# Three of four weight folds ahead of the projections, the fourth from sums and differences of mirrored channels

## The chip, the core and the metric

One NeuronCore of a Trainium2 chip runs the program. It has TensorE (PE in the profile; its weight loads are PEld), VectorE (DVE), ScalarE (ACT), GpSimd (POOL) and SyncE (SP), which issues most DMAs, 16 DMA engines, and a PSUM of eight banks. The metric is the device time of one execution in microseconds; lower is better.

## What is computed

One step of a two-layer diffusion backbone in fp32: 1024 latent and 256 context tokens of 1024 channels. Layer 0 has two attention mixers (global, and windowed with sinks), layer 1 a Fourier mixer. Cut to what matters here:

```python
def fourier_mix(u):
    b, s, _ = u.shape
    ug = u.astype(jnp.float32).reshape(b, s, C_GROUPS, C_GROUP_DIM)   # 4 groups of 256 channels
    f = jnp.fft.fft2(ug, axes=(1, 3), norm="ortho")
    return jnp.real(f).reshape(b, s, C_WIDTH).astype(u.dtype)

def odd_mix(h, w_in, w_out):
    u, gate = jnp.split(h @ w_in, 2, axis=-1)
    return (fourier_mix(u) * jax.nn.silu(gate)) @ w_out

# per layer: m = silu(cond) @ ada_w + ada_b -> shift, scale, gate
#   x = x + gate * mixer(rms_norm(x, g) * (1 + scale) + shift); at the end a final rms_norm
```

The Fourier transform along a group's 256 channels is linear in `u = h @ w_u`. So the kernel applies it to the weight: for each of the four groups it multiplies the group's 256 columns of `w_u` by a 256 x 256 table (cosines of frequencies 0 to 128, sines of 1 to 127). This is a *fold*, and its result goes to DRAM (`wd`) until layer 1 reads it.

## The kernel before, in words

All products are fp32, most of them as three products of a high and a low part (`mm3`, `F32R`). Tokens come in ten tiles of 128 rows, channels in eight blocks of 128.

**Opening.** The string `PH0` is an order written out by hand: one letter and a number for each step, carried out by `first_step`. Inside it the DMAs that SP issues keep the order of the code; the order on the other engines is that of the tile framework's scheduler, fixed when the program is built, and each engine takes its instructions in that order. `f0` and `f1` load a fold's two weight tiles (`wuT`, 2 x 512 KB, in halves) and the table `fch`; `F00` to `F13` are the pieces of folds 0 and 1; `L0` to `L3` load modulation weights, `A` multiplies them (`ada`), `M` transposes a result (`modt`) and writes `moda` and `modb`; `x` loads token groups, `N` normalises them, `T` transposes one channel block (`xt`), `X` and `Y` modulate it; `w0` loads the key/value weights, `s0` splits them, `K` and `R` are the products with them (`kv0s` to `kv6s`); `G00` to `G11` store the results of folds 0 and 1. The `t` banks of PSUM, three of them, are shared by `xt`, `modt` and the early fold pieces.

**A fold piece** (`fold_piece(g, kb2, ...)`) makes two blocks of 128 input channels. Each block is two products added up in PSUM (one for each half `j` of the 256 group channels): 128 x 128 weights from `wu[j]` (tile names `w`), and 128 x 256 of the table (tile name `h`). The four products fill one bank (`wa`), which ScalarE empties; four pieces make a fold. A product in plain fp32 is two records in the trace, one for each pass. Early pieces (`first=True`) keep their result in `u` buffers; late ones store it at once.

**Attention.** Blocks of two heads go through scores (`sL`, `sB`, `sC`), softmax, transposes (`pt`), value products (`av`) and a store to DRAM (`od`). Between blocks a `Filler` with a credit per block puts in other work: projections, gates (`ga`), at last folds 2 and 3 (named in `FLATE`, cost `FC` a piece) and the first output projections (`oz`, a token tile at a time, two halves). An output projection needs its attention output (`od`), gates (`gd`) and softmax totals (`scd`) back from DRAM, in `proj_in`, where GpSimd multiplies the three; `load_to` starts it a step ahead. After the attention (`late[0]`) the rest of the projections is drained.

**Layer 1** then runs gates (`g1E`, `g1O`), Fourier products (`u`, `pc`, `ps`) and the last projections (`of`), the last one in three pieces of columns with its norm.

Of the kernel before, what the change touches and what calls it, by code (L numbers as in the profile page):

```python
# [17 lines left out]
P = 128  # L18
# [13 lines left out]
PH0 = """f0 S0 x0 N0 f1 L0 F00 F01 F02 F03 w0 L1 F10 F11 F12 F13 x1 A0 T0 T1 s0 M0 X0 X1 T2 L2 N1 K0 K1  # L32
 A1 T3 M1 G00 G01 G10 G11 L3 X2 X3 K2 K3 Y0 R0 Y1 R1 w1 S1 T4 A2 x2 N2 Y2 T5 M2 R2 X4 Y3 X5 R3
# [7 lines left out]
EF = 2  # L41
QPRE, HOLD, AHEAD = 0, 0, 1
# [15 lines left out]
FC, XF = 1.3, False  # L58
QE_Z = ("pt", "q", "w", "u", "p")
# [5 lines left out]
FLATE = "f2 f3"  # L65
# [74 lines left out]
def hybrid_step(ctx: ExitStack, tc: tile.TileContext, I, O):  # L140
# [85 lines left out]
    craw = sm.tile([P, 8, 2], F32, name="craw", bufs=1)  # L226
    sp.dma_start(craw, I["cT"])
    act.activation(cs, craw, AF.Tanh, scale=0.5)
    dve.scalar_tensor_tensor(out=cs, in0=cs, scalar=1.0, in1=craw, op0=ALU.add, op1=ALU.mult)
    dve.tensor_scalar(cs, cs, 0.5, None, op0=ALU.mult)  # L230
    csw = take("e", (P, 8, 32))
    pool.memset(csw.a, 0.0)
    dve.tensor_copy(csw[:, :, 0:2], cs)
# [297 lines left out]

    fold = {}

    def fold_load(g, parts=1):
        if "f" not in fold:
            fold["f"] = take("h", (P, 2, 256))
            sp.dma_start(fold["f"].a, I["fch"])
        wu = [take("w", (P, 1024)) for j in range(2)]
        for h in range(parts):
            cols = slice(h * (1024 // parts), (h + 1) * (1024 // parts))  # L540
            for j in range(2):
                sp.dma_start(wu[j][:, cols], I["wuT"][(2 * g + j) * P : (2 * g + j + 1) * P, cols])
        return wu
# [7 lines left out]
    def fold_piece(g, kb2, wu, first=False):  # L551
        f = fold["f"]
        acc = bank("t" if first else "g", f"wa{g}{kb2}")
        for i in range(2):
            c0 = (2 * kb2 + i) * P
            for j in range(2):
                pe.matmul(
                    acc[:, i * 256 : i * 256 + 256], wu[j][:, c0 : c0 + P], f[:, j, :], start=j == 0, stop=j == 1
                )
# [22 lines left out]
    def small_loads(i):  # L582
# [1271 lines left out]
    sp.dma_start(O["y"][7 * P : 8 * P, 0:512], yt[:, 0:512])  # L1854
# [109 lines left out]
```

## Time and profile before

| | |
|---|---|
| median of 3 runs | 1200.98 us (1199.07 to 1201.01) |
| the profiled execution | 1199.7 us, its span 1197.9 us |
| TensorE busy | 1161.1 us |
| VectorE, ScalarE, GpSimd busy | 842.1, 578.5, 329.2 us |
| granted TensorE clock, mean | 0.992 |
| moved by DMA | 168.81 MB, 141 GB/s |

How to read the rows: an engine, the line of the kernel, the operation, and output <- input by tile names. `x` counts instructions. In an order of time the first two numbers are the start and the length in us, and `[idle <-who]` says how long the engine had been idle and what ended that. Matmul records overlap, so that their spacing and not their length is what TensorE spends. In a table of stretches each engine's busy time stands with its count, then the granted clock, the DMA share and GB/s.

### The profile page before, as it was taken

The numbers are of one execution on the slowest core, as the hardware profiler recorded it, in microseconds if no ns is written. First come the engines' busy times: TensorE is split into PE (matmuls) and PEld (weight loads), VectorE is DVE, ScalarE is ACT, GpSimd is POOL, SyncE is SP. The second block draws the span as 40 slices with busy tenths as digits, with TensorE's granted clock in tenths as the row PEclk, the third lists the DMA queues.
The fourth block names the chain that finished last, engine by engine and source line by source line (L and its number), as shares of the span: only waits on it lengthen the run. The fifth ranks groups of instructions, "written<-read, shape, count | busy, mean of one in ns | idle before, by whom it ended". The sixth has DMA issues, their size and how long they took to land. (4 is left out here: it accounts for less than half of the span.)

```text
span 1197.9 us, 22049 instructions
## 1 busy us (share of the span) xinstructions
PE 1161.1 (97%) x8103; PEld 1038.0 (87%) x8103; DVE 842.1 (70%) x2000; ACT 578.5 (48%) x1159; POOL 329.2 (27%) x298
## 2 busy tenths in 40 slices
PE   7999999999999999999999989989999999999997
PEld 5787899999999998899989979878878888997886
DVE  3479787877677776678888978688756953467543
ACT  3343465666556555556666765533463224342211
POOL 2255644411323230010110135313112217345001
PEclk9899999999999999999999999999999999999999
DMA  9957512323623232354353588576214436264321
GB/s 321 365 190 258 176 44 77 94 80 102 158 69 97 76 95 84 92 128 113 86 144 90 151 255 240 188 234 206 86 33 155 142 106 186 81 210 147 120 105 54
DMA packets 129840, 168.81 MB, mean 141 GB/s; under 512 B 26298, under 2 KB 86454, under 8 KB 129732
## 3 DMA queue, kind: packets, MB, share of 16 engines
q1 hardware_dynamic: 127364, 159.01, 43.6%
q0 software_dynamic: 2368, 8.39, 2.1%
q8 instruction: 64, 1.05, 0.4%
q14 instruction: 44, 0.36, 0.1%
HBM read 123.19 MB, written 44.16 MB: 140 GB/s over the span
## 5 line engine op out<-in xcount | busy, mean ns | idle before, releaser
L1044 DVE TENSOR_TENSOR pt<-pt,pt 128x512 fp32r<-128x512 f32 (+1 forms) x264 | 171.1, 657 | 40.6 <-ACT pt L275 39.9
L275 ACT ACTIVATE pt<-pt 128x512 fp32r<-128x512 f32 (+1 forms) x264 | 146.7, 576 | 91.2 <-PE pt L1041 53.9
L1047 PE MATMUL av<-pt,u 128*128 128x256 f32 x1008 | 165.1, 287 | 0.0
L1041 PE MATMUL pt<-identr,p 128*128 128x128 f32 x1008 | 154.9, 272 | 0.7 <-ACT e L1026 0.4
L263 PE MATMUL q<-w,u 128*128 128x256 f32 x960 | 143.7, 287 | 0.2 <-ACT h L725 0.2
L1047 PEld LDWEIGHTS av<-pt,u 128*128 128x128 f32 x1008 | 137.8, 189 | 3.1 <-DVE pt L1044 0.3
L263 PEld LDWEIGHTS q<-w,u 128*128 128x128 f32 x960 | 126.7, 189 | 5.8 <-issue 0.8
L263 PE MATMUL ga<-u,w 128*128 128x512 f32 (+1 forms) x576 | 124.5, 361 | 0.4 <-DVE h L817 0.3
L1041 PEld LDWEIGHTS pt<-identr,p 128*128 128x128 f32 x1008 | 118.9, 140 | 6.9 <-ACT e L1026 0.6
L965 ACT ACTIVATE p<-p,nm 128x1280 f32<-128x1280 f32 (+1 forms) x80 | 95.4, 1193 | 58.1 <-DVE p L958 57.8
L263 PEld LDWEIGHTS ga<-u,w 128*128 128x128 f32 x576 | 93.9, 188 | 14.6 <-ACT e L1056 0.5
L281 POOL TENSOR_TENSOR w<-h,w 128x512 fp32r<-128x512 f32 x39 | 52.3, 1357 | 129.6 <-DVE w L277 98.2
L924 PE MATMUL sL<-u,q 128*128 128x512 f32 x256 | 82.4, 409 | 0.8 <-DMA q<-qd 0.8
L281 POOL TENSOR_TENSOR u<-h,u 128x512 fp32r<-128x512 f32 x24 | 33.7, 1411 | 159.2 <-ACT u L275 148.1
L965 ACT ACTIVATE p<-p,NM 128x640 f32<-128x640 f32 (+2 forms) x80 | 59.2, 740 | 33.5 <-DVE p L958 33.2
L924 PE MATMUL sC<-u,q 128*128 128x256 f32 x320 | 62.8, 296 | 2.4 <-DMA q<-qd 1.9
L958 DVE TENSOR_SCALAR_CACHE_REDUCE p<-sL 128x512 f32<-128x512 f32 x64 | 43.8, 684 | 25.8 <-PE sL L924 16.3
L263 PE MATMUL oz<-u,u 128*128 128x512 f32 x208 | 59.5, 396 | 1.7 <-DVE h L1239 1.7
L263 PE MATMUL oz<-u,w 128*128 128x512 f32 x192 | 58.2, 396 | 0.4 <-ACT w L275 0.4
L698 POOL TENSOR_TENSOR h<-h,rope 128x512 f32<-128x512 f32 (+1 forms) x18 | 21.6, 1199 | 126.3 <-ACT h L781 77.7
L958 DVE TENSOR_SCALAR_CACHE_REDUCE p<-sL,nm 128x512 f32<-128x512 f32 x64 | 47.7, 745 | 12.0 <-PE sL L924 11.1
L924 PEld LDWEIGHTS sC<-u,q 128*128 128x128 f32 x320 | 48.3, 189 | 5.6 <-DVE e L1058 1.8
(745 smaller groups left out, 2589.2 us busy)
## 6 DMA issues: line engine op xcount, KB each, us to landing
q<-qd SPq DMA_DIRECT2D x80, 256.0 KB
p<-i_ada_w SPq DMA_DIRECT2D x20, 512.0 KB
h<-i_w_in SPq DMA_DIRECT2D x40, 256.0 KB
h<-i_w_out SPq DMA_DIRECT2D x32, 256.0 KB
pt<-i_ada_w SPq DMA_DIRECT2D x15, 512.0 KB
qd<-pt SPq DMA_DIRECT2D x20, 256.0 KB
q<-i_ada_w SPq DMA_DIRECT2D x9, 512.0 KB
qd<-q SPq DMA_DIRECT2D x18, 256.0 KB
```

The lines of the kernel that those rows point to most:

```text
L263: pe.matmul(out, a, b, start=i == 0, stop=i == n - 1)
L275: act.activation(out, in_, AF.Copy)
L281: pick("lo" + lc, lc).tensor_sub(dst_l, src, dst_h)
L698: pick("rope", XE["rope"]).tensor_mul(t1.rearrange("p t h (b c) -> p t (h b) c", b=2), y.rearrange("p t h (b c) -> p t (h b) c", b=2), cb)
L924: pe.matmul(ps, q_at(q, s, hc), keys, start=s == 0, stop=s == 1)
L958: dve.tensor_scalar(p[i][:, end[i] : end[i] + n], ps, sign, last[i], op0=ALU.mult, op1=ALU.min, accum_out=c)
L965: act.activation(p[i][:, 0 : end[i]], p[i][:, 0 : end[i]], AF.Exp, bias=last[i], scale=-1.0, accum_out=SU[:, t, hd + i, 0:1],)
L1041: pe.transpose(tp[:, jj * 256 + i * P : jj * 256 + i * P + P], p[i][:, off : off + P], ident)
L1044: dve.tensor_sub(pt[:, 1, 0:n], tp[:, 0:n], pt[:, 0, 0:n])
L1047: pe.matmul(acc, vv, pt[:, s, jj * 256 : jj * 256 + 256], start=c + jj + s == 0, stop=c + jj == nt - 1 and s == 1,)
```

## The change

Five edits go together.

1. Fold 2 moves into `PH0`: its load behind the modulation weights `L0`, its pieces `F20` to `F23` among the first transposes, its two stores (`G20`, `G21`) behind the second group's steps. `EF` is 3, so that the whole table `fch` is given up after three folds.
2. Fold 3 stays late and is made otherwise. The host orders a group's channels as 0 to 128 and then 255 down to 129, in `wuT` and in the table's rows alike, so that row p of the second tile is the mirror of row p of the first. Cosines are even and sines odd under the mirror: so the 129 cosine columns need the sum of the two tiles alone, and the 127 sine columns their difference. GpSimd makes the sum and VectorE the difference, 512 columns at a time; a block is then one product of 129 columns and one of 127. Row 0 pairs channel 0 with channel 128, whose cosines alternate in sign, so VectorE adds -2 times channel 128 (the new small input `w128`) to the odd cosine columns of each block.
3. The load and the SiLU of the conditioning vector (`craw`) come behind fold 0's load.
4. `AHEAD` goes from 1 to 2: after the attention a projection's operands are fetched two steps ahead.
5. The last of the final two stores is issued by ScalarE's queue.

```diff
-PH0 = """f0 S0 x0 N0 f1 L0 F00 F01 F02 F03 w0 L1 F10 F11 F12 F13 x1 A0 T0 T1 s0 M0 X0 X1 T2 L2 N1 K0 K1
- A1 T3 M1 G00 G01 G10 G11 L3 X2 X3 K2 K3 Y0 R0 Y1 R1 w1 S1 T4 A2 x2 N2 Y2 T5 M2 R2 X4 Y3 X5 R3
+PH0 = """f0 S0 x0 N0 f1 L0 F00 F01 F02 F03 f2 w0 L1 F10 F11 F12 F13 x1 A0 T0 T1 s0 F20 M0 F21 X0 X1 T2 F22 F23 L2 N1 K0 K1
+ A1 T3 M1 G00 G01 G10 G11 L3 X2 X3 K2 K3 Y0 R0 Y1 R1 w1 S1 T4 A2 x2 N2 Y2 T5 M2 R2 G20 G21 X4 Y3 X5 R3
   K4 Y4 K5 A3 T6 Y5 M3 R4 X6 T7 R5 X7 Y6 K6 Y7 K7 R6 R7"""
...
-EF = 2
-QPRE, HOLD, AHEAD = 0, 0, 1
+EF = 3
+QPRE, HOLD, AHEAD = 0, 0, 2
...
+E_FO, E_FW = "d", "d"
...
-FLATE = "f2 f3"
+FLATE = "f3"
...
     def fold_piece(g, kb2, wu, first=False):
         f = fold["f"]
+        if not first and kb2 % 2 == 0:
+            cols = slice(kb2 * 256, kb2 * 256 + 512)
+            fold["e"] = take("h", (P, 512))
+            pool.tensor_add(fold["e"].a, wu[0][:, cols], wu[1][:, cols])
+            pick("fo", E_FO).tensor_sub(wu[1][:, cols], wu[0][:, cols], wu[1][:, cols])
         acc = bank("t" if first else "g", f"wa{g}{kb2}")
         for i in range(2):
-            c0 = (2 * kb2 + i) * P
+            c0, b0 = (2 * kb2 + i) * P, i * 256
+            if not first:
+                ec = (kb2 % 2 * 2 + i) * P
+                pe.matmul(acc[:, b0 : b0 + 129], fold["e"][:, ec : ec + P], f[:, 0, 0:129], start=True, stop=True)
+                pe.matmul(acc[:, b0 + 129 : b0 + 256], wu[1][:, c0 : c0 + P], f[:, 0, 129:256], start=True, stop=True)
+                continue
             for j in range(2):
                 pe.matmul(
                     acc[:, i * 256 : i * 256 + 256], wu[j][:, c0 : c0 + P], f[:, j, :], start=j == 0, stop=j == 1
...
         copy("wo", "a", wo, acc.rearrange("p (i f) -> p i f", i=2))
+
+        for i in range(0 if first else 2):
+            odd = wo[:, i, 1:129:2]
+            n = 8 * g + 2 * kb2 + i
+            pick("fw", E_FW).tensor_scalar(odd, odd, w128[:, n : n + 1], None, op0=ALU.add)
...
+            sp.dma_start(w128, I["w128"])
+            dve.tensor_scalar(w128, w128, -2.0, None, op0=ALU.mult)
...
     for op in PH0.split():
         first_step(op)
+        if op == "f0":
+            cond_vectors()
...
-    sp.dma_start(O["y"][7 * P : 8 * P, 0:512], yt[:, 0:512])
+    act.dma_start(O["y"][7 * P : 8 * P, 0:512], yt[:, 0:512])
...
+    fch = fch[np.concatenate([np.arange(129), 256 - np.arange(1, 128)])].reshape(2, 128, 256).transpose(1, 0, 2)
...
-        "wuT": w1[:, :1024].T,
+        "wuT": w1[:, mirror].T,
```

Three places show how the instructions move. On TensorE in the opening, from the last transpose of the second channel block on, before (`modt0` is the first modulation transpose, `xt02` and `xt03` channel blocks 2 and 3):

```order
L424 MATMUL xt01_316<-identr_85,u9_137 128x128
L516 MATMUL modt0_329<-identr_85,e40_309 128x128
L424 MATMUL xt02_344<-identr_85,u6_134 128x128
...
L467 MATMUL ada1_407<-pt30_234,e2_114 32x128 x2
L526 MATMUL kv0s_117<-w22_222,u41_334 128x256
```

and now:

```order
L427 MATMUL xt01_323<-identr_85,u9_138 128x128
L573 MATMUL wa20_336<-h3_118,w22_223 128x256
L573 MATMUL wa20_336<-h3_118,w23_224 128x256
...
L519 MATMUL modt0_343<-identr_85,e42_316 128x128
L573 MATMUL wa21_348<-h3_118,w22_223 128x256
L573 MATMUL wa21_348<-h3_118,w23_224 128x256
...
L529 MATMUL kv0s_112<-w24_229,u44_354 128x256
```

Piece `wa20` stands ahead of `modt0` and `wa21` between it and the first key/value product; `xt02`, and behind it `wa22` and `wa23`, follow that product now.

In SP's queue at the same place, before (`p19` is the last tile of `L0`, the `h` tiles are the key/value weights, `pt30` is the first of `L1`):

```order
L496 DMA p19_194<-i_ada_w 128x4x256
L296 DMA h24_224<-i_w_in0 128x2x256
L296 DMA h25_226<-i_w_in0 128x2x256
L296 DMA h28_230<-i_w_in0 128x2x256
L296 DMA h29_232<-i_w_in0 128x2x256
L496 DMA pt30_234<-i_ada_w 128x4x256
```

and now:

```order
L499 DMA p19_195<-i_ada_w 128x4x256
L548 DMA w22_223<-i_wuT 128x512
L548 DMA w23_224<-i_wuT 128x512
...
L299 DMA h26_231<-i_w_in0 128x2x256
L299 DMA h27_233<-i_w_in0 128x2x256
```

Fold 2's four half tiles stand ahead of the key/value weights and so of everything behind them.

On TensorE late in the attention, before (`wa20` is fold 2's first piece, `pt7_31`, `av7_30` and `sB6_30` are attention blocks):

```order
L1041 MATMUL pt7_310_9298<-identr_85,p895_9063 128x128 x4
L924 MATMUL sC6_30_9371<-u683_7045,q908_9176 128x256 x2
L996 MATMUL sB6_300_9378<-u681_7043,q908_9176 128x384 x2
L557 MATMUL wa20_9277<-h919_9252,w920_9254 128x256
L557 MATMUL wa20_9277<-h919_9252,w921_9255 128x256
...
L1041 MATMUL pt7_312_9310<-identr_85,p895_9063 128x128 x4
```

and now, there and 41 rows further on:

```order
L1068 MATMUL pt7_310_9340<-identr_85,p899_9100 128x128 x4
L569 MATMUL wa30_9317<-h923_9289,h933_9314 128x129
L570 MATMUL wa30_9317<-h923_9289,w925_9292 128x127
...
L1023 MATMUL sB6_301_9430<-u685_7080,q912_9213 128x384 x2
L1068 MATMUL pt7_312_9352<-identr_85,p899_9100 128x128 x4
...
L951 MATMUL sC5_30_9709<-u687_7082,q955_9511 128x256 x2
L951 MATMUL sC5_31_9753<-u687_7082,q955_9511 128x256 x2
L266 MATMUL oz00_9569<-u826_8507,w930_9308 128x512
```

Fold 3's first piece stands where fold 2's stood, its products are 129 and 127 columns wide, and the first projection `oz00`, which stood behind the first halves of block 5's transposes and all eight late pieces, now follows the scores `sC5_31`, with four pieces ahead of it.

More of the change, by code (lines that the diff above doesn't have):

```diff
@@ L224, in hybrid_step, with cond_vectors @@
     rope = cp.tile([P, 8, 96], F32, name="rope")
[L226 to L230, printed above, removed]
     csw = take("e", (P, 8, 32))
     pool.memset(csw.a, 0.0)
-    dve.tensor_copy(csw[:, :, 0:2], cs)
+    def cond_vectors():
+        craw = sm.tile([P, 8, 2], F32, name="craw", bufs=1)
+        sp.dma_start(craw, I["cT"])
+        act.activation(cs, craw, AF.Tanh, scale=0.5)
+        dve.scalar_tensor_tensor(out=cs, in0=cs, scalar=1.0, in1=craw, op0=ALU.add, op1=ALU.mult)
+        dve.tensor_scalar(cs, cs, 0.5, None, op0=ALU.mult)
+        dve.tensor_copy(csw[:, :, 0:2], cs)
     def rsqrt(name, v, n, mul, post=None, pw=False):
@@ L532, in hybrid_step @@
     fold = {}
+    w128 = cp.tile([P, 32], F32, name="w128")
     def fold_load(g, parts=1):
         if "f" not in fold:
-            fold["f"] = take("h", (P, 2, 256))
-            sp.dma_start(fold["f"].a, I["fch"])
+            whole = parts > 1
+            fold["f"] = take("h", (P, 2 if whole else 1, 256))
+            sp.dma_start(fold["f"].a, I["fch"] if whole else I["fch"][:, 0:1, :])
         wu = [take("w", (P, 1024)) for j in range(2)]
@@ L570, in fold_piece @@
             drop(wb)
+        if not first and kb2 % 2 == 1:
+            drop(fold["e"])
         if kb2 == 3:
@@ L1880 @@
     w1 = A["odd_w_in"][0]
+    mirror = np.concatenate([256 * g + np.concatenate([np.arange(129), 256 - np.arange(1, 128)]) for g in range(4)])
     n = np.arange(256)
     ang = 2 * np.pi * ((n[:, None] * np.arange(129)[None, :]) % 256) / 256
-    fch = np.concatenate([np.cos(ang), np.sin(ang[:, 1:128])], axis=1).reshape(2, 128, 256).transpose(1, 0, 2)
+    fch = np.concatenate([np.cos(ang), np.sin(ang[:, 1:128])], axis=1)
+    fch = fch[np.concatenate([np.arange(129), 256 - np.arange(1, 128)])].reshape(2, 128, 256).transpose(1, 0, 2)
     def tab(fn, pos, p, length, scale):
@@ L1936 @@
         "cv": np.stack([A["cache_v_a"][0, 0], A["cache_v_b"][0, 0]]).reshape(2, 256, 128),
-        "wuT": w1[:, :1024].T,
+        "wuT": w1[:, mirror].T,
+        "w128": w1[:, 128:1024:256].reshape(8, 128, 4).transpose(1, 2, 0).reshape(128, 32),
         "w_g1": w1[:, 1024:][:, chan],
```

## The prediction

> **What bounds the kernel now.** I read the page first, then the stretches of the span, then the orders of time in the three places that the change touches.
>
> ```profile
> span 1197.9 us, 22049 instructions
> PE 1161.1 (97%) x8103; PEld 1038.0 (87%) x8103; DVE 842.1 (70%) x2000; ACT 578.5 (48%) x1159; POOL 329.2 (27%) x298
> PE   7999999999999999999999989989999999999997
> ```
>
> TensorE is busy for 97% of the span: work taken from it is worth its own time, unless the engine then waits. Its slices below 9 lie at the start, about the 25th and at the end. So I split the span there.
>
> ```profile
> 20.00:30.00 10.00, 7.50 (x91) 4.90 (x89) 5.44 (x9) 2.35 (x5) 3.91 (x3) 0.89 1.10 348
> 30.00:40.00 10.00, 8.67 (x89) 6.92 (x89) 2.24 (x7) 3.33 (x7) 1.65 (x1) 0.77 1.06 382
> 40.00:50.00 10.00, 8.64 (x50) 7.06 (x50) 5.80 (x10) 3.11 (x6) 3.07 (x3) 0.66 1.09 379
> 50.00:60.00 10.00, 10.00 (x140) 8.94 (x140) 4.41 (x10) 4.11 (x7) 2.95 (x2) 1.00 1.05 334
> ...
> 70.00:80.00 10.00, 9.85 (x79) 9.15 (x78) 9.15 (x18) 4.62 (x8) 5.75 (x5) 1.00 0.25 74
> ...
> 100.00:120.00 20.00, 17.80 (x241) 14.54 (x242) 19.11 (x42) 4.22 (x10) 10.53 (x11) 1.00 0.85 276
> ...
> 690.00:740.00 50.00, 46.24 (x300) 41.98 (x300) 40.48 (x105) 32.52 (x76) 21.88 (x22) 1.00 0.89 265
> 740.00:800.00 60.00, 55.95 (x291) 46.69 (x290) 45.66 (x98) 25.12 (x59) 20.01 (x13) 1.00 0.63 201
> 800.00:900.00 100.00, 97.75 (x462) 79.32 (x461) 71.85 (x117) 44.93 (x83) 20.47 (x16) 0.99 0.38 120
> ```
>
> After the length stand busy TensorE, its weight loads, VectorE, ScalarE and GpSimd, then granted clock, DMA share and GB/s. From 20 to 50 us TensorE idles 5.2 us, runs at a clock of 0.89, 0.77 and 0.66, and the DMA share is above 1. From 100 to 120 us VectorE, busy 19.1 of 20, is the bound. From 690 to 800 us, where folds 2 and 3 and the first output projections lie between attention blocks, TensorE idles 7.8 us. From 800 us on it is the bound nearly alone.
>
> **The folds.** What does one cost?
>
> ```profile
> 10.76:21.70 10.94, 10.94 (x51) 9.31 (x50) 1.00 1.07 372
> ...
> 724.42 0.60 PE L1041 MATMUL pt<-identr,p 128*128 128x128 f32 x4
> 724.85 1.89 PE L557 MATMUL wa<-h,w 128*128 128x256 f32 x8
> ...
> L557 PE MATMUL wa<-h,w 128*128 128x256 f32 x64 | 15.3, 382 | 1.7 <-ACT pt L275 1.3 <-ACT h L275 0.4
> ```
>
> The first row counts line 557 alone between 10.76 and 21.70 us, where it runs back to back at full clock: 51 records in 10.94 us, 0.2145 us each. The 382 ns in the last row are the length of a record, which overlaps the next. The last row also says that folds 2 and 3 are 64 records: 32 for a fold, that is 32 x 0.2145 = **6.9 us** of TensorE each.
>
> *Fold 2 leaves the late stage:* -6.9 us.
>
> *Fold 3 streams 129 or 127 columns instead of 256.* No row has an fp32 product of that size with 128 weights. The nearest one is the transpose, 128 fp32 weights and 128 columns: four in 724.85 - 724.42 = 0.43 us, 0.108 us each. I take that: 32 x (0.2145 - 0.108) = **-3.4 us**. The bounds are 0, if the weights, whose load lasts 9.31/50 = 0.186 us in the first row, set the pace, and -3.4 us, half the stream. I choose the transpose's end since it loads as many fp32 weights.
>
> Fold 3 pays elsewhere: two GpSimd sums and two VectorE differences of 128x512, and eight small additions on VectorE.
>
> ```profile
> 23.84 1.27 POOL L281 TENSOR_TENSOR w<-h,w 128x512 fp32r<-128x512 f32 x1 [7.33 <-DVE w L277]
> ...
> 25.76 1.63 DVE L281 TENSOR_TENSOR w<-h,w 128x512 fp32r<-128x512 f32 x1
> ...
> 27.65 0.15 DVE L479 TENSOR_TENSOR modb<-modt,bT 128x4 f32<-128x4 f32 x1
> ...
> 30.99 0.69 DVE L439 TENSOR_TENSOR u<-h,u 128x512 fp32r<-128x512 f32 x1
> ```
>
> That is 2 x 1.27 us on GpSimd and 2 x 0.69 + 8 x (0.15 to 0.43) = 2.6 to 4.8 us (a 128x4 row here, a 128x512 cast at 23.33 below) on VectorE, which is busy 40.5 of 50 us there; beside it TensorE has the attention. I cost it at 0 as long as VectorE has its 9.5 idle us; without them it is 2.6 to 4.8. Row 25.76 shows a price more: a VectorE subtraction beside a GpSimd one takes 1.63 us instead of 0.69, so each sum may hold VectorE up by 0.9 us, 1.9 us in all, which its idle time covers as well.
>
> The Trainium skill ("SBUF — State Buffer", on the shared port pair) says that the two engines' shared port pair is an exclusive lock for an instruction; that rule speaks against sums on GpSimd, and by it up to 2 x 1.27 us of VectorE would be lost. The rows agree in kind, with 0.94 us a time.
>
> **Fold 2 in the opening.** Its 6.9 us come in between the first modulation sums and the first K/V products.
>
> ```profile
> 25.47 0.33 PE L516 MATMUL modt<-identr,e 128*128 128x128 f32 x1
> 28.01 1.09 PE L424 MATMUL xt<-identr,u 128*128 128x128 f32 x4 [2.21 <-DVE moda L484]
> ...
> 29.95 0.80 PE L526 MATMUL kv0s<-w,u 128*128 128x256 f32 x2 [0.28 <-ACT u L437]
> ...
> 38.72 0.33 PE L516 MATMUL modt<-identr,e 128*128 128x128 f32 x1 [0.38 <-ACT e L511]
> 40.42 0.51 PE L526 MATMUL kv0s<-w,u 128*128 128x256 f32 x2 [1.38 <-ACT u L437]
> ...
> 42.10 1.94 PE L424 MATMUL xt<-identr,u 128*128 128x128 f32 x8 [0.93 <-DVE u L418]
> ```
>
> The gaps up to 42.1 us are 2.21 + 0.28 + 0.38 + 1.38 + 0.93 = 5.2 us. They would hide most of 6.9 us, but not for free. Piece wa20 stands ahead of modt0: 8 x 0.2145 = 1.7 us and an eviction of 0.60 us (21.82 below), so modt0 comes near 27.5, and wa21 waits in turn for VectorE to empty modt0. The loads shift too:
>
> ```profile
> 14.62 4.23 SPq L296 DMA_DIRECT2D h<-i_w_in  x4
> ...
> 23.33 0.43 DVE L277 CAST w<-h 128x512 fp32r<-128x512 f32 x1 [6.03 <-DMA h<-i_w_in]
> ...
> 21.82 0.60 ACT L275 ACTIVATE u<-wa 128x512 f32<-128x512 f32 x1 [1.13 <-PE wa L557]
> ...
> 33.54 1.06 ACT L412 ACTIVATE h<-u 128x1024 bf16<-128x1024 f32 x1 [2.97 <-DMA u<-i_x]
> ```
>
> Fold 2's 1.05 MB lie in SP's queue ahead of the key weights (issued at 14.62, waited for until 23.33) and of all behind them; at the 348 GB/s of the first stretch that is 3.0 us for everything later: the weights near 26.3, the second x group near 36.5. VectorE casts these weights ahead of the modulation (27.65 above), so moda comes 1 to 2 us later and kv0s near 31.5. The second group, reached at 42.10 now, would be reached between 42.5 and 45. Against it stands the clock: at 0.89, 0.77 and 0.66 the thirty us from 20 to 50 lose 1.1 + 2.3 + 3.4 = 6.8 us of full rate, all of it behind the two gaps that wa20 to wa23 now fill in part. So the fold costs between -2 us (both gaps filled, the clock kept, the loads hidden) and +6.9 us (nothing hidden). I take **+2.5 us**, near the 3.0 us of the loads, because the DMA share above 1 lasts until 60 us and the later loads are waited for. The four evictions (0.6 us each) fall on a ScalarE that is busy 2.35 of 10 us, and its two stores of 512 KB are issued behind the last x loads, and the DMA share is 0.25 from 70 us on; both at 0. Moving c's small load behind fold 0's brings fold 0 0.45 us forward at most, which is inside these bounds.
>
> **The late stage without its fillers.** The folds fill the time while the first projection tile is fetched.
>
> ```profile
> 690.31 0.78 POOL L1211 DMA_DIRECT2D u<-od  x1 [5.28 <-PE ga L263]
> ...
> 697.64 0.55 POOL L1214 DMA_DIRECT2D u<-gd  x1
> 707.56 2.36 POOL L1217 TENSOR_TENSOR u<-u,u 128x1024 f32<-128x1024 f32 x1 [9.37 <-DMA u<-gd]
> 710.00 2.35 POOL L1218 TENSOR_TENSOR u<-u,u 128x1024 f32<-128x1024 f32 x1
> ...
> 696.16 1.97 PE L557 MATMUL wa<-h,w 128*128 128x256 f32 x8 [1.29 <-ACT pt L275]
> ...
> 718.40 0.40 PE L924 MATMUL sC<-u,q 128*128 128x256 f32 x2
> ...
> 732.83 5.80 PE L263 MATMUL oz<-u,w 128*128 128x512 f32 x24
> ```
>
> The tile's last load is issued at 697.64, lands at 707.56, and two products on GpSimd end at 712.35; with its split it is ready near 715, and oz00 begins at 732.83: 17 us of slack. In the new order oz00 stands right behind the score products sC5_30 and sC5_31, the first of which now run at 718.40. Between wa20 (696.16) and them lie five fold pieces now, 5 x 1.72 = 8.6 us; in the new order four halved ones lie there, 4 x 0.86 = 3.5 us. So oz00 comes near 718.4 - 5.1 = 713.3, some 2 us ahead of its operands, and the next three tiles move forward with it. What waits behind a projection on TensorE is attention itself, since the engine takes its instructions in order. The waits of the four tiles are between 0 (the fetch gains as much, with fold 3's load and fold 2's stores, 2.1 MB, out of a stretch with a DMA share of 0.89) and 8 us (2 us at each); below nothing they reach by 2 us, if some of the present 7.8 us of idle closes. I take **+2.5 us**.
>
> Of AHEAD nothing in the trace gives a price: none of the gaps from 740 to 800 ends with a load. I take 0 and keep -2 (half of the 4.05 us of idle in that stretch) and +1 as ends.
>
> **The end.**
>
> ```profile
> 1194.34 0.33 SPq L1854 DMA_DIRECT2D o_y<-q  x1
> 1194.77 0.37 SPq L1853 DMA_DIRECT2D o_y<-q  x1
> ```
>
> Two stores go out one after the other from SP; with the second one on ScalarE's queue it leaves 0.43 us earlier: -0.4 us, between 0 and -0.4.
>
> **Sum.** -6.9 - 3.4 + 2.5 + 2.5 - 0.4 = -5.7 us. The profiled execution took 1199.7 us (1.8 us around its span), between the runs of 1199.07 to 1201.01; that gives **1194.0 us**.
>
> **Rivals.**
> - *The clock is kept.* The granted clock is low in just the thirty us that hold the gaps. If wa20 to wa23 fill them, the opening costs -2 instead of +2.5 us: 1189.5 us. For it: the fold lies exactly there. Against: wa20 and wa21 each bring a wait of their own. The Trainium skill ("TensorE: Matmul & The Clock Gate", on what the gate does) says that the clock halves after an idle window of some 3.4 us and returns after a busy one; the trace agrees in that the clock is low behind gaps, but its longest gap there is only 2.21 us.
> - *The opening pays in full:* VectorE bound at 100 to 120 us hands on every delay, +6.9 instead of +2.5: 1198.4 us.
> - *The narrow product is not shorter:* weights set the pace, fold 3 keeps 6.9 us: 1197.4 us. Then the change doesn't do what it is made for.
> - *Slower: projections come before their operands.* oz00, oz40, oz20 and oz60 each wait on TensorE for a fetch that needs some 17 us from its last load (697.64 to 715). A wait of 3 us at each of the four is 12 us instead of 2.5: 1203.5 us. It decides from 8.2 us of such waits on, where the whole gain is gone. For it: the last load takes 9.9 us to land. Against: the 2.1 MB that leave this stretch.
>
> **How the numbers follow.** 0.2% of 1201, or 2.4 us, is about what a measurement of this kernel can tell from no change. Forecast 0.42 (1191.5 to 1197); clock kept 0.15; opening in full 0.13 and weights 0.08, both at the edge of the gain; waits 0.12; the rest, 0.10, mixtures near no change. Faster: 0.42 + 0.15 + 0.08, half of 0.13 and 0.025 of the rest, 0.74; the same 0.14; slower the 0.12 of the waits. With every unknown at its good end the sum is -16.7 us (1183.0), with every one at its bad end +15.7 (1215.4); such ends seldom come together, so I leave out 0.06 below and 0.14, mainly the waits, above: 1187.5 to 1201 us.
>
> **What would show it.** In the changed profile: fold records of 129 and 127 columns at a spacing near 0.108 us; a granted clock above 0.8 from 25 to 48 us; the second x group's transposes no more than 3 us later than 42.1; the idle time ahead of oz00, and every landmark behind 800 us some 5 us earlier. I am wrong if the fold spacing stays near 0.2 us, if the second x group comes over 5 us later than now, or if TensorE's idle time from 690 to 800 us grows beyond 16 us.

## The result and the profile after

The changed kernel takes 1204.5 us (median of 9 runs, 1202.4 to 1206.58) against 1200.2 us before (9 runs, 1195.3 to 1201.2): 1.0034 of before, 95% interval 1.0018 to 1.0051, so **slower by some 4 us**. Forecast were 1194.0 us and a gain. The profiled execution is the fastest of the nine, 1202.4 us, 2.7 us above that of before. Two of the twelve executions of one kernel below, `plain_f3_cond_old`, ran at a granted clock of 0.75, took 1416 and 1418 us and are left out of its ratio.

The page of the changed kernel, its span, the busy line and TensorE's slices:

```profile
span 1200.5 us, 22076 instructions
PE 1155.7 (96%) x8103; PEld 1031.0 (86%) x8103; DVE 843.3 (70%) x2011; ACT 577.1 (48%) x1159; POOL 332.0 (28%) x300
PE   7999999999999999999999879998999999999997
```

TensorE is busy 5.4 us less, and the span is 2.6 us longer. To see where, the span is cut at the same five instructions in both kernels: the first transposes of a block of the second attention round (428 us), those of a late block (619 us), the last transposes of the E quarter of layer 1 (872 us), and the last piece of the last product (1188 us). They were found by counting the records of each line, since the program's order gives their number. The table of stretches of before (length, TensorE, its weight loads, VectorE, ScalarE, GpSimd, granted clock, DMA share, GB/s):

```profile
0.00:428.38 428.38, 412.59 (x3572) 383.61 (x3573) 312.81 (x760) 224.22 (x403) 152.94 (x151) 0.98 0.48 150
428.38:619.06 190.68, 189.50 (x1277) 172.93 (x1276) 140.62 (x407) 113.42 (x237) 22.55 (x18) 1.00 0.39 102
619.06:872.07 253.01, 244.59 (x1397) 211.78 (x1398) 204.96 (x477) 135.81 (x296) 64.94 (x53) 1.00 0.59 180
872.07:1188.23 316.16, 311.44 (x1837) 266.87 (x1836) 180.80 (x350) 103.25 (x221) 87.13 (x75) 0.99 0.38 124
1188.23:1197.90 9.67, 3.00 (x26) 2.79 (x24) 2.87 (x8) 1.74 (x5) 1.60 (x3) 0.86 0.15 54
```

and of the changed kernel:

```profile
0.00:427.52 427.52, 413.92 (x3605) 385.21 (x3605) 312.25 (x761) 225.67 (x407) 153.20 (x151) 1.00 0.49 155
427.52:617.50 189.98, 189.47 (x1277) 172.93 (x1276) 140.56 (x407) 113.47 (x237) 22.54 (x18) 1.00 0.39 103
617.50:876.17 258.67, 238.86 (x1366) 203.78 (x1367) 202.06 (x486) 132.09 (x290) 67.57 (x54) 0.99 0.57 167
876.17:1190.50 314.33, 310.46 (x1836) 266.29 (x1835) 185.60 (x350) 104.09 (x223) 87.13 (x75) 0.99 0.38 125
1190.50:1200.50 10.00, 3.01 (x26) 2.80 (x24) 2.88 (x8) 1.74 (x5) 1.57 (x3) 0.76 0.14 52
```

The opening, with a fold more in it, is 0.9 us *shorter*. The third stretch, from here on **the late stage**, holds the loss: 31 records fewer, and 258.67 instead of 253.01 us. TensorE idles there 258.67 - 238.86 = 19.8 us instead of 253.01 - 244.59 = 8.4.

The largest piece of that idle time, in TensorE's order of time:

```profile
703.25 1.20 PE L1074 MATMUL av<-pt,u 128*128 128x256 f32 x8
711.33 0.76 PE L951 MATMUL sC<-u,q 128*128 128x256 f32 x2 [6.88 <-DMA q<-qd]
```

A score product waits 6.9 us for a load of `q`; before, the same product (the 281st record of its kind in both kernels) waited 1.6 us, from 707.54 to 709.10. What the DMA engines were doing stands in GpSimd's order of time and the stretches of 5 us around it (the granted clock is third from the end; the last two rows are those of before):

```profile
692.03 0.78 POOL L1238 DMA_DIRECT2D u<-od  x1 [0.57 <-PE ga L266]
692.80 0.54 POOL L1255 DMA_DIRECT2D w<-i_xp  x1
693.33 0.54 POOL L1238 DMA_DIRECT2D w<-od  x1
696.30 1.07 POOL L1243 DMA_DIRECT2D u<-scd  x2
697.37 0.55 POOL L1241 DMA_DIRECT2D u<-gd  x1
697.91 0.54 POOL L1241 DMA_DIRECT2D w<-gd  x1
```

```profile
695.00:700.00 5.00, 5.00 (x45) 4.95 (x44) 4.63 (x14) 4.02 (x10) 3.38 (x5) 1.00 1.01 338
700.00:705.00 5.00, 4.45 (x36) 4.14 (x35) 5.00 (x17) 4.64 (x11) 0.00 (x0) 1.00 1.05 256
705.00:710.00 5.00, 0.00 (x0) 0.00 (x0) 1.64 (x7) 0.07 (x1) 1.72 (x1) 0.76 1.06 285
710.00:715.00 5.00, 3.67 (x19) 3.70 (x20) 2.38 (x8) 1.52 (x4) 0.61 (x1) 0.55 0.79 217
...
700.00:705.00 5.00, 5.00 (x37) 4.79 (x37) 4.80 (x17) 4.43 (x10) 0.00 (x0) 1.00 1.06 317
705.00:710.00 5.00, 3.44 (x24) 2.98 (x23) 3.43 (x9) 2.24 (x7) 2.36 (x2) 1.00 0.62 147
```

Between 692 and 698 us six loads of 0.5 MB are issued for projections (the two of `scd` counted as one), and the DMA share is at 1 until 710 us. Before, four such loads and the two of fold 3's weight tiles, the same 3.0 MB, were issued from 690 to 698 us, and the share from 705 to 710 us was 0.62. So the fetch is no larger than before, and it ends later. `q` shares it. The issue rows of `q` on SP's queue, now and before:

```profile
697.36 1.20 SPq L956 DMA_DIRECT2D q<-qd  x1
...
698.66 1.25 SPq L929 DMA_DIRECT2D q<-qd  x2
```

By the semaphore records of the traces, the load issued at 697.36 has all landed at 711.2, 13.9 us later; the second of the two before, issued at 699.30, had landed at 709.0, 9.7 us later. Measured from the first late fold product (696.40 us now, 696.16 before), TensorE reaches the score product 3.3 us sooner than before, and `q` lets it go 2.0 us later. Of the 3.3 us, 2.6 are the fold's: 24 of its records stand between in both kernels, now narrow ones (24 x (0.2145 - 0.108)). What the narrow products save ahead of this wait, the wait takes back.

And behind the idle time **the granted clock is half** (0.55 from 710 to 715 us; the clock's records say 0.5 from 707.64 to 714.46): what follows the wait runs at half speed. The narrow fold products at 713.17 us, for one, stand 0.21 us apart, against 0.11 at full clock. The Trainium skill ("TensorE: Matmul & The Clock Gate", section "What's actually happening") has the clock halve after an idle window of about 3.4 us. The trace nearly agrees: the halving comes 3.2 us into the gap. The table of TensorE's waits in the late stage shows what else has grown (the last three rows are the largest of before):

```profile
PE sC L951 <- DMA q<-qd: 6.9, 1, 6.9
PE av L1074 <- DVE e L1085: 3.2, 4, 1.2
PE oz L266 <- DVE h L1266: 3.1, 3, 1.6
PE oz L266 <- DVE e L1085: 1.6, 1, 1.6
...
PE sC L924 <- DMA q<-qd: 1.9, 2, 1.6
PE oz L263 <- DVE h L1239: 1.7, 1, 1.7
PE tt L1023 <- DVE byp L1020: 1.6, 1, 1.6
```

In such a row stand the waiting operation, what ended the wait, the us in total, the number of waits and the longest.

Value products and projections wait for VectorE to empty a bank, 7.9 us in the second to fourth row; before, the two largest waits for VectorE there were 1.7 and 1.6 us.

### The profile page after: what moved, and what is told of

Its sections match the earlier page's. It is cut to its first block, busy times and chain, and to the rows that moved or that the text cites. A ratio compares the mean times of both kernels' runs of the same rounds, so it can differ in the third digit from the quotient of the medians.

```text
span 1200.5 us, 22076 instructions
## 1 busy us (share of the span) xinstructions
PE 1155.7 (96%) x8103; PEld 1031.0 (86%) x8103; DVE 843.3 (70%) x2011; ACT 577.1 (48%) x1159; POOL 332.0 (28%) x300
## 5 line engine op out<-in xcount | busy, mean ns | idle before, releaser
L284 POOL TENSOR_TENSOR u<-h,u 128x512 fp32r<-128x512 f32 x20 | 27.0, 1355 | 143.0 <-ACT u L278 115.8
L985 DVE TENSOR_SCALAR_CACHE_REDUCE p<-sL,nm 128x512 f32<-128x512 f32 x64 | 47.7, 745 | 13.7 <-PE sL L951 13.0
L266 PE MATMUL of<-u,u 128*128 128x512 f32 x150 | 48.6, 395 | 0.4 <-DVE u L1810 0.4
## 6 DMA issues: line engine op xcount, KB each, us to landing
q<-qd SPq DMA_DIRECT2D x80, 256.0 KB
h<-i_w_in SPq DMA_DIRECT2D x40, 256.0 KB
h<-i_w_out SPq DMA_DIRECT2D x32, 256.0 KB
qd<-pt SPq DMA_DIRECT2D x20, 256.0 KB
qd<-q SPq DMA_DIRECT2D x18, 256.0 KB
```

Of the source, the lines that this page charges most:

```text
L266: pe.matmul(out, a, b, start=i == 0, stop=i == n - 1)
L284: pick("lo" + lc, lc).tensor_sub(dst_l, src, dst_h)
L985: dve.tensor_scalar(p[i][:, end[i] : end[i] + n], ps, sign, last[i], op0=ALU.mult, op1=ALU.min, accum_out=c)
```

## The experiments

Eighteen kernels ran, each in five rounds beside the kernel before. **Half clock** below is the sum of the records of a granted clock of 0.5 inside the late stage. **Work** is what the kernel has more or less than before on TensorE there, at 0.2145 us a record of 256 columns and 0.108 of a narrow one, the forecast's price. Idle is the stage's length less TensorE's busy time. The ratio is of all runs of a kernel. Stage, idle and half clock are of its one profiled execution, which lies up to 4.7 us off the median of a kernel's executions (`plain_f3_cond_old`, 1195.3 against 1200.0), so small differences in these three columns say little.

| kernel | ratio to before (95%) | work | stage | idle | half clock |
|---|---|---|---|---|---|
| before | 1 | 0 | 253.0 | 8.4 | 0 |
| changed | 1.0034 (1.0018 to 1.0051) | -10.3 | 258.7 | 19.8 | 6.8 |
| f2_opening_only | 1.0020 (1.0002 to 1.0037) | -6.9 | 253.5 | 12.0 | 10.2 |
| mirror_late_only | 1.0071 (1.0052 to 1.0090) | -6.8 | 264.5 | 19.0 | 13.7 |
| after_ahead1 | 1.0078 (1.0057 to 1.0099) | -10.3 | 263.4 | 22.3 | 17.1 |
| before_half_products | 1.0035 (1.0020 to 1.0050) | -6.9 | 255.2 | 12.5 | 10.2 |
| before_f3_twice | 1.0022 (1.0009 to 1.0035) | +6.9 | 254.5 | 4.0 | 0 |
| before_ahead2 | 1.0020 (1.0005 to 1.0034) | 0 | 252.0 | 6.4 | 0 |
| after_plain_f3 | 0.9988 (0.9975 to 1.0001) | -6.9 | 252.7 | 12.0 | 6.8 |
| plain_f3_sp | 0.9978 (0.9967 to 0.9990) | -6.9 | 253.6 | 13.4 | 3.4 |
| plain_f3_cond_old | 1.0001 (0.9980 to 1.0023) | -6.9 | 249.5 | 11.3 | 0 |
| after_wide | 1.0049 (1.0030 to 1.0067) | -6.8 | 257.9 | 16.1 | 6.8 |
| after_double_wide | 1.0053 (1.0038 to 1.0068) | -3.4 | 258.7 | 14.9 | 3.4 |
| after_late_od2 | 1.0033 (1.0014 to 1.0053) | -10.3 | 256.0 | 16.2 | 6.8 |
| after_sum_dve | 1.0062 (1.0041 to 1.0083) | -10.3 | 261.9 | 24.5 | 3.4 |
| after_no_add | 1.0045 (1.0033 to 1.0058) | -10.3 | 262.2 | 19.9 | 13.7 |
| after_no_prep | 1.0022 (1.0010 to 1.0035) | -10.3 | 256.1 | 14.9 | 13.7 |
| after_table | 1.0002 (0.9991 to 1.0013) | -8.6 | 254.1 | 14.2 | 3.4 |
| table_wide | 1.0010 (0.9995 to 1.0026) | -6.9 | 257.3 | 14.4 | 6.8 |
| plain_with_adds | 0.9981 (0.9957 to 1.0006) | -6.9 | 251.5 | 13.0 | 0 |

### Parts of the change alone, and the work alone

Fold 2 in the opening and no more, on before (with the new `PH0`):

```diff
-EF = 2
+EF = 3
...
-FLATE = "f2 f3"
+FLATE = "f3"
```

> Before, with fold 2 moved into the opening and nothing else changed (fold 3 stays a plain fold of 32 records, AHEAD 1, last store on SP). Theory 'late loads' (from 690 us on TensorE waits for q and projection loads that do not come earlier when work is taken out, so the folds were fillers): opening -0.9 us as in the trace of the changed kernel (landmarks at 420 to 600 us stand 0.9 us earlier), the late stage gives back the 6.9 us and up to 4 us more: between -2 and +3 us against before, ratio 0.998 to 1.003. Theory 'AHEAD' (the waits come from fetching two steps ahead): -0.9 - 6.9 = -7.8 us, ratio near 0.9935. Theory 'mirror' (the sums and differences on GpSimd and VectorE and the narrow products cost the time): also near 0.9935, since fold 3 is plain here.

Both late folds mirrored, nothing else (the changed kernel with these lines and `PH0` as they were before, and `cond_vectors` and the last store too):

```diff
-EF = 3
-QPRE, HOLD, AHEAD = 0, 0, 2
+EF = 2
+QPRE, HOLD, AHEAD = 0, 0, 1
...
-FLATE = "f3"
+FLATE = "f2 f3"
```

> Before, with folds 2 and 3 both late and both made from sums and differences (64 records of 129 or 127 columns), nothing in the opening, AHEAD 1, last store on SP, conditioning vector at its old place. Late loads: the 6.8 us taken from TensorE come back as waits, within 2 us of before, ratio 0.998 to 1.002. AHEAD: -6.8 us, 0.994. Mirror: slower than before by 3 us or more (twice the sums and additions of the changed kernel), 1.003 or above.

The changed kernel with AHEAD back at 1:

```diff
-QPRE, HOLD, AHEAD = 0, 0, 2
+QPRE, HOLD, AHEAD = 0, 0, 1
```

> The changed kernel with AHEAD back at 1. Late loads: the attention part is the same up to the drain behind the attention, so the 6.9 us gap ahead of a score product near 704 us stays, and the time is within 2 us of the changed kernel, 1.002 to 1.005 of before. AHEAD: the loss goes and the time falls to 0.994 to 0.997 of before.

TensorE's work alone, on before:

```diff
-            for j in range(2):
+            for j in range(2 if first else 1):
```

> Before, with the late folds 2 and 3 made from the first tile of channels alone: one product a block instead of two, so 32 records (6.9 us of TensorE) fewer between 690 and 735 us; all loads, evictions and stores stay. It leaves out the half of these two folds that comes from the second tile. TensorE as the bound, which the forecast assumed: -6.9 us, 0.994. Late loads: the time comes back as waits for q and projection loads, within 2 us of before, 0.998 to 1.002.

The last is the plainest test of the forecast's base. Its late stage, from the table of stretches:

```profile
618.03:873.21 255.18, 242.65 (x1365) 207.57 (x1366) 197.51 (x477) 135.59 (x295) 65.59 (x52) 0.98 0.61 178
```

With 6.9 us of products taken out and no other work changed, the kernel is 0.35% *slower*. TensorE's busy time falls by only 244.59 - 242.65 = 1.9 us, with 10.2 us now at half clock, and idle grows by 4.1 us. So **taking TensorE work out of the late stage did not shorten it**; "TensorE as the bound" falls.

The edit changes one thing more than the work. The scheduler builds the order anew for each program, and TensorE's order in the late stage moves. From the first late fold product to the first record of `oz`, the trace of before has 156 records of the attention (`sB`, `sC`, `pt`, `av`); that of `before_half_products` has 94, that of the changed kernel 84, and all seventeen kernels with less late work than before have 72 to 102. So whenever work goes, the first projections move forward between the attention blocks. Whether the loss comes from the missing work or from this new order, no run here separates; only the two runs on before that take nothing out (`before_ahead2`, `before_f3_twice` below) keep the 156.

Fold 2 in the opening, with its 6.9 us gone from the stage, leaves the stage as long as before (253.5). Mirroring both late folds costs 0.71%, as only the theory "mirror" had it; but that theory had `f2_opening_only` at 0.9935, which is 1.0020. AHEAD at 1 makes the changed kernel slower still (1.0078), so AHEAD was no cause of the loss; that theory falls. "Late loads" was right for `f2_opening_only` alone and too low for the other three (0.998 to 1.002 for the mirrored folds and the halved products, 1.002 to 1.005 for AHEAD at 1), so it is a part of the account at most.

### AHEAD alone, a plain fold 3, and superfluous products

```diff
-QPRE, HOLD, AHEAD = 0, 0, 1
+QPRE, HOLD, AHEAD = 0, 0, 2
```

> Before with AHEAD at 2 and nothing else. The run with AHEAD back at 1 stood at 1.0078 of before against 1.0034 for the whole change, so AHEAD 2 is worth some 5 us inside the change. Theory 'a gain of its own': -4 to -5 us here too, 0.996. Theory 'it only repairs waits that the change makes': before has no idle of TensorE from 800 to 880 us, so there is nothing to repair, 0.999 to 1.001.

A plain fold 3 in the changed kernel (the branch for the mirrored products goes, the whole table is loaded, and the sums, differences and additions go):

```diff
-            whole = parts > 1
+            whole = True
...
-                pe.matmul(acc[:, b0 : b0 + 129], fold["e"][:, ec : ec + P], f[:, 0, 0:129], start=True, stop=True)
-                pe.matmul(acc[:, b0 + 129 : b0 + 256], wu[1][:, c0 : c0 + P], f[:, 0, 129:256], start=True, stop=True)
-                continue
```

> The changed kernel with fold 3 as a plain fold (32 records of 256 columns, no sums, differences and additions); fold 2 in the opening, AHEAD 2 and all else as changed. TensorE as the bound: 3.4 us slower than the changed kernel, 1.006 of before. Mirroring costs more than it saves (late fillers gone, idle and half clock in their place): faster than the changed kernel, 0.998 to 1.002 of before, with less than 6 us of half clock and less idle between 690 and 880 us.

Superfluous products in front of the mirrored ones:

```diff
+                pe.matmul(acc[:, b0 : b0 + 256], wu[1][:, c0 : c0 + P], f[:, 0, :], start=True, stop=True)
                 pe.matmul(acc[:, b0 : b0 + 129], fold["e"][:, ec : ec + P], f[:, 0, 0:129], start=True, stop=True)
                 pe.matmul(acc[:, b0 + 129 : b0 + 256], wu[1][:, c0 : c0 + P], f[:, 0, 129:256], start=True, stop=True)
```

> The changed kernel with a third, superfluous product of 256 columns ahead of each block's two narrow ones in fold 3: TensorE does as many columns as in a plain fold (+3.5 us), all the sums, differences, additions and buffers of the mirrored fold stay. TensorE as the bound: 3.5 us slower than the changed kernel, 1.006 of before. Fillers (the time taken out is idle anyway): within 1.5 us of the changed kernel or below it, at most 1.0045. If the sums, differences and buffers are what costs: the same as the changed kernel, and the kernel with a plain fold 3 well below both.

> As the one with the superfluous product, but with two of them a block: 7 us of TensorE more than in the changed kernel, about what fold 2 took late. TensorE as the bound: 7 us slower than the changed kernel, 1.009 of before. Fillers: the idle ahead of the score product at 704 us (6.9 us) shrinks by as much as lies ahead of it, and the time stays within 2.5 us of the changed kernel, at most 1.0055.

The late stages of the two and of the plain one:

```profile
617.73:875.64 257.91, 241.86 (x1382) 208.58 (x1382) 197.22 (x487) 133.20 (x292) 67.20 (x54) 0.99 0.57 167
```

```profile
619.69:878.42 258.73, 243.83 (x1397) 209.89 (x1398) 200.09 (x487) 133.97 (x292) 67.02 (x54) 0.99 0.57 167
```

```profile
617.66:870.35 252.69, 240.67 (x1365) 206.78 (x1366) 194.48 (x476) 131.93 (x290) 65.47 (x52) 0.99 0.58 172
```

Seven us of useless products leave the stage at 258.7 us, as it was; idle shrinks from 19.8 to 14.9, and the kernel's ratio goes from 1.0034 to 1.0053, some 2 us for 7 us of work. With a plain fold 3 the stage is 6 us shorter although TensorE has 3.4 us more to do. So, with the other edits in place, the loss against before is **all in the mirrored fold**: with a plain one the kernel is at 0.9988 (its half clock, 6.8 us, is not the less than 6 that was expected). AHEAD 2 on before gains nothing (1.0020, even a little above the 0.999 to 1.001 that was expected): little idle time is there to fill.

### What to fill with, and what else could hold the stage up

Buffers of the third projection (the same for `gl` and `rl`; `last` takes the buffer dropped last):

```diff
-            ol = take(OB[0], (P, 8, P))
+            ol = take(OB[0], (P, 8, P), last=r == 2)
```

> The changed kernel with one thing else: the operand buffers of the third projection (token tile 2) are taken from those dropped last, so that its 0.5 MB of attention output, which the changed kernel fetches at 693.33 us between the loads of the first tile, comes behind the second tile's. Theory 'crowded fetch' (with the mirrored fold this load got ahead of the q load of the score product at 704 us and of the first tile's gates): the 6.9 us of idle ahead of that product shrink by 2 us or more, the half clock behind it goes, and the time falls by 3 to 5 us, to 0.999 to 1.001 of before. Theory 'the sums and additions themselves' (VectorE and GpSimd work in the way of the attention): no change, 1.002 to 1.005 of before.

```diff
-            pool.tensor_add(fold["e"].a, wu[0][:, cols], wu[1][:, cols])
+            dve.tensor_add(fold["e"].a, wu[0][:, cols], wu[1][:, cols])
```

> The changed kernel with the two sums of 128x512 on VectorE instead of GpSimd, where they stand ahead of the first projection loads. Theory 'sums on GpSimd hold up its load queue, and VectorE beside them': the loads leave 1.5 us earlier and the time falls by 2 to 4 us, 1.000 to 1.002 of before. Theory 'crowded fetch': the third tile's load stays ahead, no change beyond 1.5 us, 1.002 to 1.005 of before.

The plain fold 3 with `cond_vectors()` called ahead of `PH0`:

> The kernel with a plain fold 3 (0.9988 of before), with the conditioning vector back at its old place, ahead of fold 0's load. If that place costs the opening something (the run with fold 2 in the opening and the old place stood 4.1 us late at 428 us, those with the new place -0.9 to +2.6 us): 2 to 3 us slower, 1.001. If that spread is only where the windows of half clock fall: 0.998 to 1.000.

Before, with fold 3's products twice:

```diff
-            for j in range(2):
+            for j in range(4 if g == 3 else 2):
```

> Before with all products of fold 3 made twice, 6.9 us of TensorE more between 715 and 740 us. TensorE as the bound of the late stage: +6.9 us, 1.0057. Waits for loads and softmax as the bound (fillers): within 1.5 us, at most 1.0015. With the halved products at +4 us, the late stage would then have its least time near the filling that before has.

The late stage of the last:

```profile
620.67:875.16 254.49, 250.46 (x1429) 217.73 (x1430) 197.87 (x477) 135.82 (x295) 65.73 (x52) 1.00 0.59 179
```

Twice the products of fold 3 on before cost 1.5 us of the stage and 2.6 us of the time, for 6.9 us of work, between the two expectations. The first `oz` keeps its place here, so this is the price of late TensorE time with the order nearly kept: under half of its length. Before stands near its least, with less work on one side (+4 us for -6.9) and more on the other both slower. Loading the third tile's attention output later (the 693.33 row above) cut the wait ahead of the score product from 6.9 to 4.5 us and left the time where it was (1.0033): the crowded fetch is part of that gap and not the loss. The sums on VectorE made things worse (1.0062, idle 24.5), so taking them off GpSimd is no remedy; VectorE then has more to do, and what GpSimd's share costs by itself this run doesn't show. The old place of the conditioning vector gave 1.0001, between its two expectations.

### Which part of the mirrored fold

```diff
-        for i in range(0 if first else 2):
+        for i in range(0):
             odd = wo[:, i, 1:129:2]
```

> The changed kernel without the eight additions of 128x64 in fold 3; it leaves out the contribution of channel 128 to the odd cosine columns. Theory 'additions' (two of them took 2.85 us of VectorE beside a GpSimd product, ahead of a softmax that TensorE then waits for): 3 us or more faster than the changed kernel, 0.999 to 1.001 of before. Theories 'sums and differences' and 'missing TensorE time': as the changed kernel, 1.002 to 1.005.

The same, and in place of the sum and the difference the loaded tiles:

```diff
-                pe.matmul(acc[:, b0 : b0 + 129], fold["e"][:, ec : ec + P], f[:, 0, 0:129], start=True, stop=True)
+                pe.matmul(acc[:, b0 : b0 + 129], wu[0][:, c0 : c0 + P], f[:, 0, 0:129], start=True, stop=True)
```

> The changed kernel without additions, sums and differences: the narrow products of fold 3 take the loaded tiles as they are, so the mirrored sums are left out of the computation and TensorE still has its 3.4 us less. Theory 'sums and differences': 5 us faster than the changed kernel, as the one with a plain fold 3, 0.998 to 1.000. Theory 'missing TensorE time' (idle in its place, half clock behind it): as the changed kernel, 1.002 to 1.005. Theory 'additions': as the one without additions.

No additions, and a table `fce` whose first tile has 0 and whose second has 1 at row 0's odd cosine columns:

```diff
-                pe.matmul(acc[:, b0 : b0 + 129], fold["e"][:, ec : ec + P], f[:, 0, 0:129], start=True, stop=True)
-                pe.matmul(acc[:, b0 + 129 : b0 + 256], wu[1][:, c0 : c0 + P], f[:, 0, 129:256], start=True, stop=True)
+                pe.matmul(acc[:, b0 : b0 + 256], wu[1][:, c0 : c0 + P], f[:, 1, :], start=True, stop=False)
+                pe.matmul(acc[:, b0 : b0 + 129], fold["e"][:, ec : ec + P], f[:, 0, 0:129], start=False, stop=True)
```

> The changed kernel with the additions replaced by TensorE: a table of its own takes row 0's odd cosine columns from the difference, so that a block is a product of 256 columns and one of 129 (1.7 us of TensorE more in all, no additions on VectorE). Additions: as without them, 0.999 to 1.001 of before. Otherwise as the changed kernel, 1.002 to 1.005.

The plain fold 3 with the last store on SP:

> The kernel with a plain fold 3 (0.9988 of before) with the last store on SP again. The time from the last product piece to the end was 9.7 us in the runs with SP and 10.0 in those with ScalarE's queue: 0.3 us less, 0.9975 to 0.9995 of before.

The same as with the table, the second product 256 columns wide (with zeros); and the plain fold with the additions:

> The kernel with the table in place of the additions, with both products of a block 256 columns wide: fold 3 takes TensorE as long as a plain fold, with sums and differences and without additions. Theory 'missing TensorE time': as with a plain fold 3, 0.997 to 1.0005 of before. Theory 'sums and differences' (they hold up the softmax and the loads): 1.002 or above. Theory 'additions': as with a plain fold 3.

> The kernel with a plain fold 3 and, on top, the eight additions of 128x64 on VectorE; it adds a correction that a plain fold does not need, so channel 128 counts wrongly in the odd cosine columns. Theory 'additions': 1.002 or above, against 0.998 to 0.999 without them. Theories 'missing TensorE time' and 'sums and differences': as without them, 0.997 to 1.0005.

The late stage with narrow products and nothing else of the mirrored fold:

```profile
619.24:875.30 256.06, 241.21 (x1366) 207.53 (x1367) 193.03 (x477) 134.02 (x293) 64.88 (x53) 0.97 0.56 169
```

Two readings are clear and one is likely. The additions alone cost nothing that shows (0.9981 with them on a plain fold; taking them out of the changed kernel gains nothing). The narrow products alone, without sums and additions, are slower than wide ones, 1.0022 against 0.9978 and 0.9988: 4 to 5 us for 3.4 us of work less, with 13.7 us at half clock (0.97 in the row) instead of 3.4 and 6.8. The sums and differences alone, at full width, probably cost 0.2 to 0.3%: 1.0010 against 0.9988 and 0.9978, with an interval that overlaps the first one's and just misses the second's. With sums and without additions the kernel is faster with 385 or 512 columns a block than with 256 (1.0002 and 1.0010 against 1.0045). With the additions it is not (1.0034, 1.0049, 1.0053 for 256, 512 and 768). Why that is stays open; each edit also changes the order in which the scheduler puts the stage's instructions, and these runs don't separate that.

## Why the forecast was wrong, by its own steps

**The step that failed** is the sum's treatment of the late stage: "-6.9 us" and "-3.4 us" as time on the path, with "+2.5 us" for all waits that take their place. The work did go (31 records fewer in the stage). But the stage is 5.7 us longer, where the three terms make -7.8. The difference has two parts: idle grew by 11.4 us, against 2.5 taken and 8 as the bound, and TensorE's busy time fell by 5.7 us instead of 10.3, with 6.8 us of the stage at half clock. The second part was not in the sum at all: the clock was weighed as a gain in the opening, never as a loss in the late stage. What makes the idle grow when work goes, the missing work or the order that goes with it, stays open.

The same shows in all the profiles. If busy time is that of before plus the table's work plus half of the time at half clock, it comes out within 2.3 us in every run of the table: for `before_half_products` 244.6 - 6.9 + 5.1 = 242.8 (measured 242.65), for `before_f3_twice` 251.5 (250.46), for `after_no_prep` 241.1 (241.21), for the changed kernel 237.7 (238.86). So the stage's length is about work, plus idle, plus half of the half-clocked time; **about half or more of what is taken out of the first comes back in the other two, often more than all of it**. For 6.9 us less, the stage went from 253.0 to between 249.5 and 257.3. This is a fit and not a mechanism: of the changed kernel's 6.8 us at half clock TensorE is busy for 3.1 (711.33 to 714.46), which explains some 1.6 of the 4.6 us of busy time that did not go.

*The slower rival* had the size and not the place: its 1203.5 us are near the measured 1204.5 by luck. Its 12 us of waits are 11.4 of idle more, but it put them at `oz` waiting for its operands to be fetched. The first and longest is a score product that waits for `q`, while the fetch of the projections crowds it; `oz` waits 5.6 us in all, each time for VectorE. And `oz00`, forecast near 713.3 us, ahead of its operands, came at 721.52, behind that wait (732.83 before).

*The signs of being wrong* that the forecast named did not come: the spacing was right, the second x group in time, and the idle from 690 to 800 us grew from 7.8 to 11.4 us, below the 16. Of the stage's 19.8 us of idle 8.4 lie outside that stretch, 5.3 of them behind 800 us, where before had none. The landmark that did tell was the one behind 800 us: it came 4.1 us later (876.17 against 872.07) instead of some 5 sooner.

*Spacing of the narrow products.* Right: 0.108 us were taken, 0.11 measured.

```profile
696.40 0.39 PE L569 MATMUL wa<-h,h 128*128 128x129 f32 x2
...
697.07 0.39 PE L570 MATMUL wa<-h,w 128*128 128x127 f32 x2
```

Six records lie between the two starts, (697.07 - 696.40) / 6 = 0.112 us. The rival of the weights' pace is out.

*Fold 2 in the opening.* +2.5 us were taken, between -2 and +6.9; it is near 0, and "the clock is kept" was the better case:

```profile
20.00:30.00 10.00, 7.56 (x90) 5.45 (x88) 3.20 (x6) 2.07 (x4) 2.52 (x2) 1.00 1.08 359
30.00:40.00 10.00, 9.92 (x74) 8.39 (x77) 2.90 (x7) 5.69 (x10) 2.96 (x3) 1.00 1.06 377
40.00:50.00 10.00, 9.38 (x135) 7.57 (x124) 6.93 (x16) 4.75 (x9) 4.34 (x4) 1.00 1.09 364
...
42.62 0.41 PE L427 MATMUL xt<-identr,u 128*128 128x128 f32 x2 [0.41 <-DVE moda L487]
```

The clock is 1.00 where it was 0.89, 0.77 and 0.66, and the second x group is reached 0.5 us later than before. That the opening comes out near 0 is not luck of one execution: the instruction at 428.38 us in before comes at 428.8 on average in the five profiled openings without the fold (427.3 to 430.1) and at 428.6 in thirteen with it and the conditioning vector behind fold 0's load (427.0 to 430.9). Before 600 us, the half clock is 12.3 us on average in the five and 4.5 in the thirteen, at half speed up to 3.9 us of work won back; the first stretch also has 13.6 us of idle time instead of 15.8. In the order with the vector at its old place there are only two profiles, 432.5 and 427.5: open.

*VectorE's cover, cost 0.* Right for the additions, probably wrong for the sums and differences (0.2 to 0.3%).

*AHEAD, 0 between -2 and +1.* Taken out of the changed kernel it costs 0.44%, some 5 us, which is outside; put into before it gains nothing. Its price depends on idle time being there.

*The last store, -0.4 us.* Not seen. The two stores now go out together, and the end comes no sooner:

```profile
1196.63 0.39 ACTq L1881 DMA_DIRECT2D o_y<-q  x1
1196.65 0.33 SPq L1880 DMA_DIRECT2D o_y<-q  x1
```

From the later issue to the span's end are 1200.5 - 1196.65 = 3.9 us, against 1197.9 - 1194.77 = 3.1 before, so that the last stretch is 10.0 instead of 9.7 us. In the twenty profiles it is 10.0 us, give or take 0.05, in all thirteen with ScalarE's queue, and 9.7 in five of the seven with SP (10.2 in `plain_f3_sp`, 11.0 in `mirror_late_only`): no gain, and rather 0.3 us lost.

## What to carry to other kernels

Work taken from the busiest engine pays only where this engine alone sets the pace. A busy share does not tell: TensorE was busy for 97% of the span and for 97% of the late stage too (244.59 of 253.01 us), and taking work from that stage made it longer. The test is cheap: take the work out, results aside, and see whether the time falls; put work in as well (`before_f3_twice`), which here left the order of the rest nearly as it was. Where a scheduler builds the order, compare that too. In these traces an idle gap also cost what followed it, at half clock, so that useful work which fills gaps elsewhere (here fold 2 in the opening) can be nearly free, while removing late work cost 4 us where it took 6.9 out. The best version found moves fold 2 and leaves fold 3 plain: 0.9978 (0.9967 to 0.9990), and 0.9988 with the last store on ScalarE's queue; 1.0001 with the conditioning vector at its old place besides. That is a gain of 0.2% at best.

## What the runs showed of the hardware

Kernels with the same order of instructions differ in where the half-clock windows fall. `after_plain_f3` and `plain_f3_sp` differ in the queue of the last store alone; their spans are 1196.8 and 1199.0 us, with 10.2 us at half clock in each before 880 us but at other places. That these places make the difference of 2.2 us is not shown. The windows are 3.4 us long or a multiple of it in every trace (the one that the end cuts aside). They do not need a gap of that length: in `plain_f3_sp` one begins at 763.2 us, and in the 3.4 us ahead of it TensorE was busy for 1.14 us. A landmark in a single profile of this kernel is good to some 2 us (427.0 to 430.9 us in the thirteen above), and terms below that have to come from many.

A VectorE addition of 128x64 can take eleven times its time. From the view of one line (least, median, longest in ns), and the row in time with the GpSimd product beside it:

```profile
L588 DVE TENSOR_SCALAR h<-h,w x8: 239/242/2682, 700.3 to 718.1; 128x64 f32<-128x64 f32 x8
...
715.52 2.85 DVE L588 TENSOR_SCALAR h<-h,w 128x64 f32<-128x64 f32 x2 [1.01 <-ACT h L278]
715.76 2.38 POOL L1245 TENSOR_TENSOR u<-u,u 128x1024 f32<-128x1024 f32 x1
```

One takes 2.68 us instead of 0.24 while a GpSimd product of 2.38 us runs, about the sum of the two. The Trainium skill ("SBUF — State Buffer", section "Who interferes with whom") has a VectorE `tensor_scalar` in a two-port mode and a GpSimd operation exclude each other for a whole instruction. This row agrees with that; which mode the addition ran in, no run here shows.
